# A decoder layer on one core: the mixer's steps in another order, weight splits and softmax scaling moved from GpSimd to VectorE, and one evacuation put behind the root

## The chip, the cores and the metric

The kernel runs on one NeuronCore of a Trainium2 chip. The metric is the device time of one execution in microseconds (us); the figure compared is the median of several runs. A profile of one execution shows when each instruction ran on TensorE (PE: matmuls; PEld: its weight loads), VectorE (DVE), ScalarE (ACT), GpSimd (POOL) and SyncE (SP, which issues the transfers).

## The reference

One layer on 256 tokens of width 1024, all in 32-bit floats:

```python
x = x + 0.5 * rmsnorm(swiglu(rmsnorm(x, g1), w_gate, w_up, w_down), post1)      # FFN 1, width 2816
h = rmsnorm(x, g2); q, k, v, p = split(h @ w_in)                                # 8 heads of 64, 512 pool channels
attn = softmax(q k^T / 8 - slope * (i - j), causal) v                           # 256 tokens are one block
pool = (mean of the last 2, 4, 8, 16 tokens - token) @ pool_w, * pool_scale     # 4 groups of 128 channels
x = x + rmsnorm([attn, pool] @ w_out, post2)
x = x + rmsnorm(cross_attention(rmsnorm(x, g3), rmsnorm(mem, g4)), post3)       # 4 heads of 256, 256 memory rows
x = x + 0.5 * rmsnorm(swiglu(rmsnorm(x, g5), ...), post4)                       # FFN 2
```

## The kernel before

All products with weights run as three matmuls of a rounded 32-bit kind: weights and activations are each split into a high part (rounded) and a low part (the rest), and high x high, high x low and low x high are added up in PSUM. The weights come as units of 8 tiles of 128x128, in the order in which they are used. `Weights._make` does a unit: ACT casts the raw unit to its high part (L79), and DVE or POOL subtracts it from the raw one (L80, the *split*, tiles `wlo<-wraw,whi`). In the FFNs every split is DVE's. Between them (mixer and cross-attention) every third unit, by `u % 3` (L76), goes to POOL, unless a written-out pace names the engine, as in the last seam. A unit is made four to five units ahead of its use.

PE's order is the order of the program. The other engines' order is found by a scheduler at build time, except in stretches between two `seam` marks, where it is the order of the code too. Each engine runs its instructions strictly in that order.

**The seams.** After each sub-layer's last product, the output's two halves of 512 columns lie in PSUM for each of two blocks of 128 tokens. `row_sums` (L312) squares each half on ACT (L322, with a sum) and multiplies it by a gain into `y` on DVE (L323). `row_root` (L328) takes the root on ACT (L330) and a reciprocal on DVE (L331). `row_add` (L338) adds y, scaled, to the residual `xt` on DVE (L339). PE transposes `xt` (L345), and ACT and DVE write the next input's high (L366, `x_hi`) and low halves (L370, `x_lo`). In the first two seams (into the mixer, into the cross-attention) PE has a pair of memory-key columns as filler between the transpositions; in the last one (into FFN 2) it has none, and the chain goes by small pieces (`ahead`, L413). Then a group of four column blocks starts (L230 low weights, L235 and L237 high weights with high and low input).

**The mixer** (from L867 on). A `pair` is two column blocks of `w_in` (L176 to L178) into the two halves of one PSUM bank (48 matmuls). After the query group, the order is: pool columns 15 and 14, the spread of the norm (L285, then `rBx`), pool columns 13 and 12, keys 4 and 5, keys 6 and 7. Then self-attention, between four blocks `vv` of the values' columns (L263 to L265): scores of two heads at a time (`self_scores`, L636, plain 32-bit float matmuls into two `small` PSUM buffers), their softmax (`self_softmax`: bias L643, maxima L645 and L646, L647, exponentials on ACT L648 and L649, and, put off to the next unit, reciprocal L652 and scaling L653 on DVE and L654 on POOL), the transposition of each head (`self_turn`, L660 to L662, copied by ACT, L663). `pool_windows` (L682) forms the trailing sums on POOL (L693 to L698), reading a DVE product (L686); `pool_out` multiplies by the pool weights (L703). The output projection `w_out` runs in eight steps (`row_step`, L297 to L299); `self_values` (L669, L671) of two heads stands behind each of the first four steps.

PSUM has eight banks: two `small`, six accumulators.

Of the kernel before, what the change touches and what calls it, by code (L numbers as in the profile page):

```python
# [15 lines left out]
P = 128  # L16
# [31 lines left out]
class Weights:  # L48
# [21 lines left out]
    def _make(self, u, engine=None):  # L70
        self._load(u)
        raw = self.raw[u]
        hi = self.pools["hi"].tile([P, UNIT * P], F32R, name="whi")
        lo = self.pools["lo"].tile([P, UNIT * P], F32R, name="wlo")
        if engine is None:
            ffn = self.tiles[u * UNIT][0].startswith("ffn")  # L76
            engine = "dve" if ffn or u % 3 else "pool"
        eng = self.nc.gpsimd if engine == "pool" else self.nc.vector
        self.nc.scalar.copy(hi, raw)  # L79
        eng.tensor_tensor(lo, raw, hi.bitcast(F32), op=ALU.subtract)  # L80
        self.split[u] = (hi, lo)
        self._load(u + 1)
        self._load(u + 2)
# [56 lines left out]
def build(nc, io, tiles_only=False):  # L140
# [170 lines left out]

    def row_sums(parts, ks, ws, t, factor):  # L312

        ys = st["ys"]
        s = tmp([P, 8], "fs")
        last = len(HALVES) - 1
        for i, d in enumerate(HALVES):
            for j, (k, w) in enumerate(zip(ks, ws)):
                row_product(parts(k), st["acc"], 0, False, j == len(ks) - 1, t, d, w)
            a = st["acc"][t][i]  # L320
            q = tmp([P, 512], "q")
            nc.scalar.activation(q, a, AF.Square, accum_out=s[:, i:i + 1])  # L322
            nc.vector.scalar_tensor_tensor(ys[:, t, d], a, factor, st["post"][:, d], op0=ALU.mult, op1=ALU.mult)  # L323
            if i == 0:
                nc.vector.tensor_scalar(s[:, 4:5], s[:, 0:1], 1.0 / D, EPS, op0=ALU.mult, op1=ALU.add)
        return s, last
# [33 lines left out]
    def row_end(parts, ks, weights, factor, nxt, pre, fillers):  # L360
# [12 lines left out]
        def products():  # L373
            st["w"].pace = [(LEAD, None)] * (LATE - 1) + [(LEAD - 1, None)]
            ws = [st["w"].get(UNIT) for _ in ks]
            st["w"].flush()
            st["ys"] = keep([P, 2, D], "y")
            r = row_root(row_sums(parts, ks, ws, 0, factor))
            st[nxt] = xsplit()
            st["xsum"] = tmp([P, 2, 2], "xsum")  # L380
            for d in HALVES:
                row_add(0, d, r)
            box["sums"] = row_sums(parts, ks, ws, 1, factor)
            x_turn(0, range(4), small)
            x_turn(0, range(4, 8), small)

        def middle():
# [6 lines left out]
            for c in range(ND):  # L394
                x_hi(0, c)
            for i in range(4):
                row_add(1, quarter(i), r)
# [15 lines left out]
        def ahead():  # L413
# [9 lines left out]
            x_lo(0, 1)  # L423
            x_lo(1, 1)

        def before(j):
# [202 lines left out]

    def self_scores(c):  # L630
        ps = [small("sc"), small("sc")]
        for lo, n, m in ((P, S, 0), (0, P, S)):
# [7 lines left out]
    def self_softmax(h, ps):  # L640
# [10 lines left out]
        def finish():  # L651
            nc.vector.reciprocal(m[:, 6:8], m[:, 4:6])  # L652
            nc.vector.tensor_scalar(s[:, :S], s[:, :S], m[:, 6:7], None, op0=ALU.mult)  # L653
            nc.gpsimd.tensor_tensor(s[:, S:], s[:, S:], m[:, 7:8].to_broadcast([P, P]), op=ALU.mult)  # L654
        defer(finish)
# [8 lines left out]

    def self_values(c):
        po, v = small("po"), st["v"]
        for h in (2 * c, 2 * c + 1):
# [14 lines left out]
    def pool_windows(g):  # L682
        W = S + PAD
        a = st["pin", g]
        aw = st["ps"][:, 4 + g, :S]
        nc.vector.tensor_tensor(a[:, PAD:], st["pps", g], st["rBx"], op=ALU.mult)  # L686
# [165 lines left out]
    def from_ffn1(parts, ks, weights):  # L852
        def to_mid():
# [14 lines left out]
    seam(False)  # L868
    pair("w_in", "xs_mix", [15 * P, 14 * P], lambda ps: (pool_in(3)(halves(ps)[0]), pool_in(2)(halves(ps)[1])),
         lambda: side(x_root))  # L870
    table(AF.Exp)
    side(x_spread)

    def q_out():
        pool_windows(3)
        pool_windows(2)
        for i, ps in enumerate(held["q"]):
            scaled_pair("qk", 2 * i, ps)

    def enter_mix():  # L880
# [3 lines left out]

    def pool_more(ps):
        for g in (1, 0):
            pool_in(g)(halves(ps)[1 - g])
            pool_windows(g)
    pair("w_in", "xs_mix", [13 * P, 12 * P], pool_more, lambda: side(q_out))
    for i in (4, 6):  # L890
        pair("w_in", "xs_mix", [i * P, (i + 1) * P], lambda ps, i=i: scaled_pair("qk", i, ps))
    side(self_scores, 0)
    fill(vv)
    side(self_scores, 1)
    fill(vv)
    side(self_turn, 0, accum)
    side(self_turn, 1, accum)
    fill(vv)
    side(self_scores, 2)
    fill(vv)  # L900
    side(self_scores, 3)
    side(self_turn, 2, accum)
    side(self_turn, 3, accum)
    side(pool_out, 3)
    k = K.pop(0)
    pr.add(*k[0])
    side(pool_out, 2)
    side(self_turn, 4)
    side(pool_out, 1)
    side(self_turn, 5)  # L910
    side(pool_out, 0)
# [9 lines left out]
    for j, k in enumerate(order[:ND - LATE]):  # L921
        pr.add(lambda k=k, j=j: row_step(st["xs_mixo"], k, j == 0), w_out(k))
        if j == 0:
            side(k_flush)
        if j < 4:
            side(self_values, j)
    seam(True)
# [167 lines left out]
```

## Time and profile before

| | us |
|---|---|
| median of 3 runs | 584.61 (583.85 to 585.74) |
| the profiled execution | 585.12 |
| its span, first to last instruction | 583.2 |
| PE busy | 569.8 (98%) |
| DVE busy | 397.3 (68%) |
| ACT busy | 341.4 (59%) |
| POOL busy | 68.8 (12%) |

PE's granted clock is full in all 40 slices of the span. The span and its 1.9 us surroundings make the execution's time. A busy share is a mean over all stages; what a wait of PE costs is read from PE's timeline at that place, where each row has start, duration, engine, line, tiles and, in brackets, the idle time of the engine ahead of it and what ended that.

### The profile page before, as it was taken

Reading aid. Unit: us, or ns where it says so; the run is one execution under the profiler, and the core shown is the slowest. Engines: PE = TensorE matmul, PEld = TensorE weight load, DVE = VectorE, ACT = ScalarE, POOL = GpSimd, SP = SyncE. Lnnn points to the kernel's source line nnn. Section 1 sums busy time; section 2 is a strip of 40 time slices with the busy share of each in tenths; the row PEclk is TensorE's granted clock in tenths of the full one; section 3 lists DMA queues with packets and bytes.
Section 4 is the critical chain, followed back from the end, with each engine's and each line's share of the span. In section 5 each row is a group of like instructions: output and inputs, shape, how many; then the busy total and the mean of one; then the engine's idle time right before and its main releaser. Section 6 shows DMA issues by size and latency. Waiting matters only on the chain.

```text
span 583.2 us, 8490 instructions
## 1 busy us (share of the span) xinstructions
PE 569.8 (98%) x3288; PEld 494.4 (85%) x3288; DVE 397.3 (68%) x634; ACT 341.4 (59%) x619; POOL 68.8 (12%) x63
## 2 busy tenths in 40 slices
PE   8999999999999999999999999999999999999995
PEld 7888888888888899778799988879888888888884
DVE  5499667777776857784377567367796766766654
ACT  6688665555555476476369457358674555555433
POOL 0000000000001126833214311101000000000001
PEclk9999999999999999999999999999999999999999
DMA  8986675556455346434336634426665555545402
GB/s 263 348 348 221 232 264 203 181 180 209 158 212 149 120 179 239 159 131 144 145 109 219 221 139 145 144 73 217 217 226 183 204 176 186 203 162 213 145 0 73
DMA packets 29833, 107.04 MB, mean 184 GB/s; under 512 B 2144, under 2 KB 3936, under 8 KB 29408
## 3 DMA queue, kind: packets, MB, share of 16 engines
q1 hardware_dynamic: 29360, 105.29, 51.7%
q10 hardware_dynamic: 432, 1.20, 0.6%
q8 instruction: 26, 0.43, 0.3%
q14 instruction: 15, 0.12, 0.1%
HBM read 105.44 MB, written 1.05 MB: 183 GB/s over the span
## 4 chain that ended last, share of the span: by engine, by line
PE 84%; ACT 4%; DMA 4%; DVE 3%; POOL 2%; issue 2%; SPq 0%; ACTq 0%; DVEq 0%; POOLq 0%
PE acc L550 13%; PE sm L550 12%; PE acc L297 10%; PE acc L298 10%; PE acc L299 10%; PE acc L549 6%; PE sm L549 6%; DMA wraw<-w 3%; ACT whi L79 2%; PE acc L176 2%; PE acc L178 2%; PE acc L177 2%; PE acc L263 1%; PE acc L265 1%; PE acc L264 1%
## 5 line engine op out<-in xcount | busy, mean ns | idle before, releaser
L80 DVE TENSOR_TENSOR wlo<-wraw,whi 128x1024 fp32r<-128x1024 f32 x164 | 204.9, 1253 | 82.6 <-ACT whi L79 82.2
L79 ACT CAST whi<-wraw 128x1024 fp32r<-128x1024 f32 x184 | 192.2, 1051 | 62.7 <-PE acc L299 36.9
L550 PE MATMUL acc<-xs,whi 128*128 128x512 f32 x320 | 114.6, 398 | 0.0
L550 PE MATMUL sm<-xs,whi 128*128 128x512 f32 x320 | 114.3, 397 | 0.0
L549 PE MATMUL acc<-xs,wlo 128*128 128x256 f32 x320 | 89.9, 281 | 0.4 <-DVE wlo L80 0.4
L549 PE MATMUL sm<-xs,wlo 128*128 128x256 f32 x320 | 90.0, 281 | 0.0
L80 POOL TENSOR_TENSOR wlo<-wraw,whi 128x1024 fp32r<-128x1024 f32 x20 | 48.7, 2435 | 313.9 <-ACT whi L79 300.0
L550 PEld LDWEIGHTS sm<-xs,whi 128*128 128x128 f32 x320 | 60.1, 188 | 14.8
L550 PEld LDWEIGHTS acc<-xs,whi 128*128 128x128 f32 x320 | 60.1, 188 | 14.3
L297 PE MATMUL acc<-whi,h 128*128 128x512 f32 x176 | 69.7, 396 | 0.0
L298 PE MATMUL acc<-wlo,h 128*128 128x512 f32 x176 | 69.5, 395 | 0.0
L299 PE MATMUL acc<-whi,h 128*128 128x512 f32 x176 | 69.3, 394 | 0.0
L549 PEld LDWEIGHTS acc<-xs,wlo 128*128 128x128 f32 x320 | 60.4, 189 | 2.1 <-DVE wlo L80 0.7
L549 PEld LDWEIGHTS sm<-xs,wlo 128*128 128x128 f32 x320 | 60.5, 189 | 0.0
L176 PE MATMUL acc<-xs,wlo 128*128 128x256 f32 x160 | 46.0, 288 | 0.0
L178 PE MATMUL acc<-xs,whi 128*128 128x256 f32 x160 | 45.3, 283 | 0.0
L177 PE MATMUL acc<-xs,whi 128*128 128x256 f32 x160 | 45.3, 283 | 0.0
L554 ACT COPY cmb<-sm 128x256 f32<-128x256 f32 x40 | 14.9, 371 | 48.8 <-PE sm L550 48.7
L554 ACT COPY cmb<-acc 128x256 f32<-128x256 f32 x40 | 14.9, 371 | 48.2 <-PE acc L550 47.9
L299 PEld LDWEIGHTS acc<-whi,h 128*128 128x128 f32 x176 | 33.0, 187 | 8.1
L298 PEld LDWEIGHTS acc<-wlo,h 128*128 128x128 f32 x176 | 33.0, 188 | 7.9
L297 PEld LDWEIGHTS acc<-whi,h 128*128 128x128 f32 x176 | 33.0, 188 | 6.6
(165 smaller groups left out, 935.4 us busy)
## 6 DMA issues: line engine op xcount, KB each, us to landing
wraw<-w SPq DMA_DIRECT2D x91, 1024.0 KB, 4.9
post<-post SPq DMA_DIRECT2D x4, 512.0 KB, 4.8
wraw<-w SPq DMA_DIRECT2D x7, 256.0 KB, 4.8
wraw<-w SPq DMA_DIRECT2D x2, 512.0 KB, 6.4
xt<-xt ACTq DMA_DIRECT2D x1, 1024.0 KB, 6.1
y<-memt SPq DMA_DIRECT2D x1, 1024.0 KB, 7.7
y<-mem SPq DMA_DIRECT2D x1, 1024.0 KB, 7.0
y<-x SPq DMA_DIRECT2D x7, 128.0 KB, 4.1
```

Source lines behind the costliest of these rows:

```text
L79: self.nc.scalar.copy(hi, raw)
L80: eng.tensor_tensor(lo, raw, hi.bitcast(F32), op=ALU.subtract)
L176: nc.tensor.matmul(o, lo, X[:, :S], start=first, stop=False, skip_group_check=True)
L177: nc.tensor.matmul(o, hi, X[:, :S], start=False, stop=False, skip_group_check=True)
L178: nc.tensor.matmul(o, hi, X[:, S:], start=False, stop=last, skip_group_check=True)
L263: nc.tensor.matmul(box[t], a, hi, start=k == 0, stop=False)
L297: nc.tensor.matmul(o, a, hi, start=first, stop=False, skip_group_check=True)
L298: nc.tensor.matmul(o, a, lo, start=False, stop=False, skip_group_check=True)
L299: nc.tensor.matmul(o, b, hi, start=False, stop=last, skip_group_check=True)
L549: nc.tensor.matmul(ps[:, S:], lo, x[:, :S], start=k == 0, stop=False, skip_group_check=True)
L550: nc.tensor.matmul(ps, hi, x, start=False, stop=k == ND - 1, skip_group_check=True)
L554: nc.scalar.copy(c, ps[:, S:])
```

## The change

Five parts:

1. Weight splits: the rule `u % 3` goes; without a named engine DVE does every split. The pace of the last seam still names POOL for one unit.
2. The scaling of the near half of a softmax (128x128) goes from POOL to DVE.
3. In the seams, for the second block of tokens, the evacuation of the second half into `y` is put off: behind the root and the first two row updates (seams with fillers), or behind the small pieces of `ahead` (last seam). The end of the kernel does not use it.
4. The mixer's order: keys first (4 and 5, then 6 and 7), scores of four heads in one visit, pool columns 15 and 14, the scores of the other four heads, pool columns 13 and 12, then the value blocks with the transpositions between them. All four groups of values stand in one visit behind the first step of `w_out`. The second two heads of each visit use accumulators instead of `small` buffers.
5. The pool's scaled copy gets two buffers of its own instead of a place in the softmax tile.

```diff
-        if engine is None:
-            ffn = self.tiles[u * UNIT][0].startswith("ffn")
-            engine = "dve" if ffn or u % 3 else "pool"
         eng = self.nc.gpsimd if engine == "pool" else self.nc.vector
...
-    def row_sums(parts, ks, ws, t, factor):
+    def row_sums(parts, ks, ws, t, factor, later=None):
...
-            nc.vector.scalar_tensor_tensor(ys[:, t, d], a, factor, st["post"][:, d], op0=ALU.mult, op1=ALU.mult)
+
+            def scaled(a=a, d=d):
+                nc.vector.scalar_tensor_tensor(ys[:, t, d], a, factor, st["post"][:, d], op0=ALU.mult, op1=ALU.mult)
+            if i == last and later is not None:
+                later.append(scaled)
+            else:
+                scaled()
...
-            for i in range(4):
+            for i in range(2):
+                row_add(1, quarter(i), r)
+            box["later"][0]()
+            for i in range(2, 4):
                 row_add(1, quarter(i), r)
...
-            nc.gpsimd.tensor_tensor(s[:, S:], s[:, S:], m[:, 7:8].to_broadcast([P, P]), op=ALU.mult)
+            nc.vector.tensor_scalar(s[:, S:], s[:, S:], m[:, 7:8], None, op0=ALU.mult)
...
-        aw = st["ps"][:, 4 + g, :S]
+        aw = st["self"].tile([P, S], F32, name="aw", bufs=2)
...
-    pair("w_in", "xs_mix", [15 * P, 14 * P], lambda ps: (pool_in(3)(halves(ps)[0]), pool_in(2)(halves(ps)[1])),
-         lambda: side(x_root))
+    pair("w_in", "xs_mix", [4 * P, 5 * P], lambda ps: held.update(k=ps), lambda: side(x_root))
...
+    side(q_out)
+    pair("w_in", "xs_mix", [6 * P, 7 * P], lambda ps: scaled_pair("qk", 6, ps))
+    side(self_scores, 0, small)
+    side(self_scores, 1, accum)
+    pool_pair(3)
+    side(self_scores, 2, small)
+    side(self_scores, 3, accum)
+    pool_pair(1)
     fill(vv)
     side(self_turn, 0, accum)
     side(self_turn, 1, accum)
     fill(vv)
-    side(self_scores, 2)
-    fill(vv)
-    side(self_scores, 3)
     side(self_turn, 2, accum)
     side(self_turn, 3, accum)
+    fill(vv)
     side(pool_out, 3)
+    side(pool_out, 2)
+    fill(vv)
+    side(self_turn, 4)
+    side(self_turn, 5)
...
         if j == 0:
             side(k_flush)
-        if j < 4:
-            side(self_values, j)
+            for c in range(4):
+                side(self_values, c, accum if c % 2 else small)
```

Three places show what that does to the engines' own order. The first is PE at the values: `po` and, in the changed kernel, `sm` and `acc` are the PSUM buffers of a group of two heads. Before, one group and then the next step of the projection:

```order
L299 MATMUL acc<-whi,xs 128x512
L669 MATMUL po<-ps,v 64x256
L671 MATMUL po<-ps,v 64x128
L669 MATMUL po<-ps,v 64x256
L671 MATMUL po<-ps,v 64x128
L297 MATMUL acc<-whi,xs 128x512
```

and of the change, two of the four groups that now follow each other:

```order
L678 MATMUL sm<-ps,v 64x256
L680 MATMUL sm<-ps,v 64x128
L678 MATMUL sm<-ps,v 64x256
L680 MATMUL sm<-ps,v 64x128
L678 MATMUL acc<-ps,v 64x256
L680 MATMUL acc<-ps,v 64x128
L678 MATMUL acc<-ps,v 64x256
L680 MATMUL acc<-ps,v 64x128
```

What moved: the other three groups came up to the first one, from behind the next three steps.

The second is DVE in the last seam, where `fs` is the root of the second block of tokens. Before:

```order
L323 SCALAR_TENSOR_TENSOR y<-acc,post 128x512
L331 RECIPROCAL fs<-fs 128x1
L339 SCALAR_TENSOR_TENSOR xt<-y,fs,xt 128x128 x2
L370 SCALAR_TENSOR_TENSOR xs<-sm,gain,xs 128x128
L339 SCALAR_TENSOR_TENSOR xt<-y,fs,xt 128x256
```

and of the change:

```order
L335 RECIPROCAL fs<-fs 128x1
L343 SCALAR_TENSOR_TENSOR xt<-y,fs,xt 128x128 x2
L374 SCALAR_TENSOR_TENSOR xs<-sm,gain,xs 128x128
L343 SCALAR_TENSOR_TENSOR xt<-y,fs,xt 128x256
L374 SCALAR_TENSOR_TENSOR xs<-acc,gain,xs 128x128
L374 SCALAR_TENSOR_TENSOR xs<-sm,gain,xs 128x128
L374 SCALAR_TENSOR_TENSOR xs<-acc,gain,xs 128x128
L323 SCALAR_TENSOR_TENSOR y<-acc,post 128x512
```

What moved: the evacuation `y` of the second half went from ahead of the reciprocal to behind the first low halves.

The third is DVE in the mixer, at the evacuation of the pool columns (`pin`, one group each; in the changed kernel `pin_2580` and `pin_2592` are those of columns 13 and 12). Before, the first two stand right behind the norm's spread, ahead of the queries' scaling:

```order
L80 TENSOR_TENSOR wlo<-wraw,whi 128x1024 x2
L686 TENSOR_TENSOR pin_2254<-acc,rBx 128x256
L686 TENSOR_TENSOR pin_2256<-acc,rBx 128x256
L801 TENSOR_TENSOR qk<-acc,rBx 128x512 x2
L80 TENSOR_TENSOR wlo<-wraw,whi 128x1024
L686 TENSOR_TENSOR pin_2354<-acc,rBx 128x256
```

and of the change, the last two, among the scalings of the last heads:

```order
L77 TENSOR_TENSOR wlo<-wraw,whi 128x1024
L661 RECIPROCAL mx<-mx 128x2 x2
L695 TENSOR_TENSOR pin_2580<-acc,rBx 128x256
L662 TENSOR_SCALAR ps<-ps,mx 128x256
L663 TENSOR_SCALAR ps<-ps,mx 128x128
L662 TENSOR_SCALAR ps<-ps,mx 128x256
L663 TENSOR_SCALAR ps<-ps,mx 128x128
L695 TENSOR_TENSOR pin_2592<-acc,rBx 128x256
```

What moved: the pool's evacuations now stand behind the softmax of the heads whose scores were formed ahead of them.

## Rows read from the trace of the kernel before

**Rows 1.** The page's costliest groups: name, tiles, count | busy us, mean ns | idle

```profile
L80 DVE TENSOR_TENSOR wlo<-wraw,whi 128x1024 fp32r<-128x1024 f32 x164 | 204.9, 1253 | 82.6 <-ACT whi L79 82.2
L79 ACT CAST whi<-wraw 128x1024 fp32r<-128x1024 f32 x184 | 192.2, 1051 | 62.7 <-PE acc L299 36.9
```

**Rows 2.** Timeline of PE in the mixer: start us, duration us, instruction, [idle before]

```profile
221.43 0.37 PE L176 MATMUL acc<-xs,wlo 128*128 128x256 f32 x1
...
238.88 0.92 PE L636 MATMUL sc<-qk 64*128 64x256 f32 x8
...
246.18 0.39 PE L265 MATMUL acc<-whi,xs 128*128 128x512 f32 x1
247.83 0.33 PE L660 MATMUL acc<-const,ps 128*128 128x128 f32 x1 [1.26 <-POOL ps L654]
...
255.40 0.39 PE L265 MATMUL acc<-whi,xs 128*128 128x512 f32 x1
256.52 1.38 PE L636 MATMUL sc<-qk 64*128 64x256 f32 x8 [0.74 <-DVE ps L643]
```

**Rows 3.** Timeline of PE at the first visit for the values

```profile
269.62 0.39 PE L298 MATMUL acc<-wlo,xs 128*128 128x512 f32 x1
269.85 0.39 PE L299 MATMUL acc<-whi,xs 128*128 128x512 f32 x1
270.16 0.66 PE L669 MATMUL po<-ps,v 128*64 128x256 f32 x4
...
270.97 0.50 PE L297 MATMUL acc<-whi,xs 128*128 128x512 f32 x1
271.31 0.40 PE L298 MATMUL acc<-wlo,xs 128*128 128x512 f32 x1
```

**Rows 4.** Timeline of PE at the three seams

```profile
204.29 0.39 PE L237 MATMUL acc<-xs,whi 128*128 128x256 f32 x1 [0.87 <-DVE xs L370]
...
301.50 0.34 PE L237 MATMUL acc<-xs,whi 128*128 128x256 f32 x1
...
388.82 0.56 PE L345 MATMUL acc<-const,xt 128*128 128x128 f32 x2 [1.18 <-DVE xt L339]
```

**Rows 5.** Timeline of DVE at the three seams

```profile
200.35 2.59 DVE L80 TENSOR_TENSOR wlo<-wraw,whi 128x1024 fp32r<-128x1024 f32 x1 [0.77 <-ACT whi L79]
...
297.75 2.35 DVE L80 TENSOR_TENSOR wlo<-wraw,whi 128x1024 fp32r<-128x1024 f32 x2
...
301.06 0.34 DVE L370 SCALAR_TENSOR_TENSOR xs<-acc,gain,xs 128x128 fp32r<-128x128 f32 x1
...
387.53 0.69 DVE L323 SCALAR_TENSOR_TENSOR y<-acc,post 128x512 f32<-128x512 f32 x1 [1.21 <-ACT q L322]
388.14 0.15 DVE L331 RECIPROCAL fs<-fs 128x1 f32<-128x1 f32 x1
388.32 0.61 DVE L339 SCALAR_TENSOR_TENSOR xt<-y,fs,xt 128x128 f32<-128x128 f32 x2
```

**Rows 6.** Timeline of POOL: two weight splits and a window step

```profile
199.45 2.41 POOL L80 TENSOR_TENSOR wlo<-wraw,whi 128x1024 fp32r<-128x1024 f32 x1 [14.22 <-ACT whi L79]
...
226.63 0.64 POOL L695 TENSOR_TENSOR win<-win 128x270 f32<-128x270 f32 x1
...
243.24 2.40 POOL L80 TENSOR_TENSOR wlo<-wraw,whi 128x1024 fp32r<-128x1024 f32 x1
```

**Rows 7.** Timeline of ACT at the last seam

```profile
387.53 0.29 ACT L330 ACTIVATE fs<-fs 128x1 f32<-128x1 f32 x1
```

**Rows 8.** Timeline of DVE in the softmax

```profile
243.40 2.26 DVE L647 TENSOR_SCALAR mx<-mx 128x2 f32<-128x2 f32 x1
...
255.92 1.01 DVE L643 SCALAR_TENSOR_TENSOR ps<-sc,const 128x384 f32<-128x384 f32 x2
...
258.15 0.55 DVE L643 SCALAR_TENSOR_TENSOR ps<-sc,const 128x384 f32<-128x384 f32 x1
...
259.45 0.34 DVE L653 TENSOR_SCALAR ps<-ps,mx 128x256 f32<-128x256 f32 x1
```

More of the change, by code (lines that the diff above doesn't have):

```diff
@@ L382, in products @@
                 row_add(0, d, r)
-            box["sums"] = row_sums(parts, ks, ws, 1, factor)
+            box["later"] = []
+            box["sums"] = row_sums(parts, ks, ws, 1, factor, box["later"])
             x_turn(0, range(4), small)
@@ L424, in ahead @@
             x_lo(1, 1)
+            box["later"][0]()
         def before(j):
@@ L626, in last_rows, with self_scores @@
         pr.add(run, weights)
-    def self_scores(c):
-        ps = [small("sc"), small("sc")]
+    def self_scores(c, alloc):
+        ps = [alloc(), alloc()]
         for lo, n, m in ((P, S, 0), (0, P, S)):
@@ L663, in self_turn, with self_values @@
         nc.scalar.copy(s, pt[:, :3 * P])
-    def self_values(c):
-        po, v = small("po"), st["v"]
+    def self_values(c, alloc):
+        po, v = alloc(), st["v"]
         for h in (2 * c, 2 * c + 1):
@@ L874, in q_out @@
     def q_out():
-        pool_windows(3)
-        pool_windows(2)
         for i, ps in enumerate(held["q"]):
             scaled_pair("qk", 2 * i, ps)
+        scaled_pair("qk", 4, held["k"])
     def enter_mix():
@@ L883, in build, with pool_pair, done @@
     side(enter_mix)
[L885 to L892, printed above, removed]
-    fill(vv)
-    side(self_scores, 1)
+    def pool_pair(g):
+        def done(ps):
+            for i in (g, g - 1):
+                pool_in(i)(halves(ps)[g - i])
+                pool_windows(i)
+        pair("w_in", "xs_mix", [(12 + g) * P, (11 + g) * P], done)
+    side(q_out)
[6 more added lines that the diff above has]
+    pool_pair(1)
     fill(vv)
@@ L898, in build @@
     fill(vv)
-    side(self_scores, 2)
-    fill(vv)
-    side(self_scores, 3)
     side(self_turn, 2, accum)
     side(self_turn, 3, accum)
+    fill(vv)
     side(pool_out, 3)
+    side(pool_out, 2)
+    fill(vv)
+    side(self_turn, 4)
+    side(self_turn, 5)
     k = K.pop(0)
     pr.add(*k[0])
-    side(pool_out, 2)
-    side(self_turn, 4)
     side(pool_out, 1)
-    side(self_turn, 5)
     side(pool_out, 0)
```

## The prediction
> **What bounds the kernel now.** I read the page first: TensorE (PE) is busy in every slice and its granted clock is full, so the time is PE's own work plus the few places where PE waits. I then listed PE's waits by length and opened the timeline of PE around each, and of the engine that ended it. The costliest groups give two prices used throughout: a weight unit costs ScalarE (ACT) 1.05 us for the cast and VectorE (DVE) 1.25 us for the split [rows 1].
>
> The mixer holds the two longest waits that this change can touch [rows 2]. The first transposition of a head begins at 247.83, 1.65 us after the last matmul ahead of it (246.18); its wait ended on GpSimd's (POOL's) scaling of that head. The last score visit begins at 256.52, 1.12 us after 255.40; it waited for a PSUM buffer that DVE had not yet read. Between 32-bit float matmuls and the rounded ones there is also a price for each crossing [rows 3]: matmuls of 512 columns follow each other at 0.23 us, but the values begin 0.31 us after the last one (269.85 to 270.16), and the one that comes after them takes 0.34 (270.97 to 271.31). A visit thus costs at least 0.08 + 0.11 = 0.19 us beside its own work. Then the seams [rows 4]: PE waits 0.87 us for DVE at 204.29, nearly nothing at 301.50, and 1.18 at 388.82.
>
> **Mix seam, at 200.** Before the first product that needs the low half, DVE works through four low halves, the splits, four more low halves and one more. Here one of two splits is POOL's, and DVE's own took 2.59 us instead of 1.25, ending 1.08 us after POOL's (199.45 + 2.41 = 201.86) [rows 5, 6]. In the next seam both splits are DVE's: from 297.75 to the end of the low half at 301.40, 3.65 us [rows 5]. The change makes the first seam like the second. DVE was free at 200.35 - 0.77 = 199.58; the deferred half of y (below) makes that 199.93, plus 3.65 is 203.58. PE follows such a low half by 0.05 to 0.1 (301.40 to 301.50), so it starts at about 203.63 instead of 204.29. Gain 0.66; bounds 0.3 and the wait itself, 0.87.
>
> **Half of y behind the root.** Before, DVE starts y (387.53), and the reciprocal stands behind it at 388.14, though ACT's root was done at 387.53 + 0.29 = 387.82 [rows 5, 7]. With y moved, the reciprocal can start at about 387.86, 0.28 us earlier, and in the last seam the first row update (388.32) and PE's 388.82 come 0.28 earlier; y then fits into DVE's idle time before the next high halves. In the two seams with fillers the same move costs: DVE now stands idle for the root (0.29 + 0.04) while y, 0.61 us, stays in front of the low halves. The end of the chain is about 0.33 later. In the mix seam this is counted above; in the next one PE's 301.50 followed 301.40 at once, so it is lost: +0.30 there (bounds 0 and 0.35). The other move of that seam, a third split on DVE before the first y, finds DVE idle.
>
> **Mixer order and POOL.** Scaling on DVE stands right behind the reciprocal. In the new order a head's transposition comes a whole pool pair and more after its softmax: three pairs take 238.88 - 221.43 = 17.45 us, so a pair is 5.8 [rows 2]. The POOL queue, with 2.4 us splits in front of the scaling, is gone: the 1.65 us go back to 0.31, -1.34. The scores use four buffers at a visit (two small, two accumulators), and the second visit is a pair later: 1.12 to 0.31, -0.81. Visits: eleven before (four scores, one merged with transpositions; three more with transpositions; four values), nine now. Two fewer at 0.19 is -0.38, at most twice that with the slower first and last matmul of a visit; I take -0.4.
>
> **Load of DVE.** Nineteen splits (one stays with POOL by a written-out order in the last seam) and eight scalings come to DVE, 19 x 1.25 = 24 us over some 210 us. Part of that is given back. At 243.40 DVE took 2.26 us for a 128x2 multiplication, ending with POOL's split (243.24 + 2.40), where two score rows of 384 columns took 1.01 together [rows 6, 8]. In the cross-attention DVE's cost is hidden: PE has no wait there, and a unit is made four to five ahead of its use, some 11 to 13 us.
>
> The Trainium skill, page "SBUF — State Buffer", section "Who interferes with whom", states that a DVE instruction of two SBUF inputs, or of a 2-port mode such as tensor_scalar, and a GpSimd one exclude each other, "the loser fully blocks". This trace agrees, with 2.26 us for the small multiplication and 2.59 for the split. By that rule the gain from POOL's splits stands, but the pooling windows stay on POOL and now run during the softmax and its new scaling on DVE; that is the second rival.
>
> **Sum.** -0.66 - 0.28 + 0.30 - 1.34 - 0.81 - 0.40 = -3.19. The profiled execution took 585.12 us (span 583.2 and 1.9 around it): 581.93. It lay 0.51 above the median of 584.61, so 581.4 us.
>
> **Rivals.** *A new wait in the transpositions.* The fourth head's transposition needs the accumulator of the second pool pair, which DVE frees only with its last evacuation of it, behind eight softmaxes. PE's way from the first score to there: 2 x (1.8 + 5.8) for scores and pairs, two value blocks of 12 x 0.23 + 0.2, a transposition visit and a half (about 1.5): 22.7 us. DVE's way: a cast and a split stand in front, 2.3; then per four heads two blocks of 2.23 (255.92 to 258.15), four scalings of some 0.6 (0.34 for the wide one) [rows 8], a split and two evacuations of 0.35: 2 x 9.0 = 18. Slack 2.4 us. Some 13 DVE instructions in that stretch exclude POOL's window steps of 0.64 us [rows 6]; half a step each is 4 us if POOL never rests, 2 if it rests half the time. So the wait lies between 0 and 1.6; with 1.2 the time is 582.6. For it: the order; against: the share of POOL's rest.
>
> *DVE becomes the bound of the mixer, slower.* The same place: if DVE stands for POOL's windows nearly in full (14 wide steps of 0.64 and small ones, some 10 us) instead of interleaving, it comes 10 us late, less 2.4 of slack: +7.6, or 589. It decides from a lateness of 2.4 + 3.2 + 1.75 = 7.3 us on. For it speaks that DVE took 2.26 us for a 128x2; against, that this was one long POOL instruction, while window steps are short and let DVE in between.
>
> *The waits only move.* The 2.15 us of the two mixer waits reappear at another buffer or transposition, since the same softmax must be done by the same DVE. Then only seams and visits are left, -1.04: 583.6. Against it: the new order puts some 15 us between a score and its use, the old one had 5 to 9.
>
> **How the numbers follow.** Forecast 581.4: 0.62; new wait 582.6: 0.18; only moved 583.6: 0.13; DVE bound 589: 0.07. About 0.3%, 1.75 us, can be told from no change, so faster means below 582.86. The forecast's own bounds (mix seam 0.3 to 0.87, lost seam 0 to 0.35, visits 0.2 to 0.8) give 580.5 to 582.0, and the runs scatter by about 0.9 either way: 579.9 to 582.8 for it alone. Adding the third case, 579.9 to 583.7. Faster: 0.60 + 0.12 + 0.03 = 0.75; same 0.17; slower 0.08.
>
> **What would show it.** Right: no PE wait over 0.3 us between the end of the query group and the last seam; PE's 0.87 in the mix seam down to about 0.2; a new one of 0.3 in the next seam; 1.18 in the last one down to 0.9; no DVE multiplication of 128x2 above 1 us. Wrong: a PE wait at the transpositions that ends on DVE's pool evacuation (first rival), PE waiting for weight splits or scores with DVE without idle time (second), or PE waits of 2 us in the mixer that end on other buffers (third). The visits are wrong if the sum of PE's time from the first score to the end of the values, waits taken off, does not fall by 0.2 us or more.

## The result and the profile after

The changed kernel took 579.51 us (median of 4 runs, 578.48 to 579.67) beside 585.11 for the kernel before (583.85 to 585.74): ratio 0.9901 [0.9886, 0.9916], faster by 5.6 us. The forecast was 581.4, a gain of 3.2 us, with a range of 579.9 to 583.7: the direction was right, the gain is some 1.75 times the forecast one, and the time lies 0.4 us below the range. The profiled execution took 579.55 us, span 577.6.

First the waits of PE over the whole span: line, what it waited for, us in total, times, longest.

```profile
PE warm L476 <- DVE cmb L473: 1.2, 1, 1.2
PE acc L232 <- ACT whi L108: 1.0, 1, 1.0
PE acc L349 <- DVE xt L343: 0.9, 1, 0.9
PE acc L558 <- DVE wlo L77: 0.7, 1, 0.7
PE acc L234 <- DVE xs L374: 0.5, 2, 0.3
PE acc L227 <- ACT xs L370: 0.2, 1, 0.2
```

Neither of the two mixer waits is left: no line is a transposition (L669 now) or a score (L645). The first two and the fourth line lie at the start and in the first FFN; the third and the last are the last seam; the fifth is one wait of 0.25 us in each of the other two seams. PE's timeline in the mixer shows the same (start us, duration us; it answers to [rows 2]).

```profile
234.01 0.28 PE L175 MATMUL acc<-xs,whi 128*128 128x256 f32 x1
234.22 0.92 PE L645 MATMUL sm<-qk 64*128 64x256 f32 x8
234.97 0.82 PE L645 MATMUL acc<-qk 64*128 64x256 f32 x8
...
244.09 0.39 PE L262 MATMUL acc<-whi,xs 128*128 128x512 f32 x1
244.32 0.27 PE L669 MATMUL acc<-const,ps 128*128 128x128 f32 x1
...
247.50 0.39 PE L262 MATMUL acc<-whi,xs 128*128 128x512 f32 x1
247.73 0.27 PE L669 MATMUL acc<-const,ps 128*128 128x128 f32 x1
```

A transposition starts 0.23 us after the matmul ahead of it, the spacing of two matmuls of 512 columns; before it was 1.65. The second score visit, now behind matmuls of 256 columns, starts 0.21 us after the last of them; the late one before started 1.12 us after its own.

The one visit for all values (answers to [rows 3]):

```profile
265.23 0.39 PE L296 MATMUL acc<-whi,xs 128*128 128x512 f32 x1
265.55 0.66 PE L678 MATMUL sm<-ps,v 128*64 128x256 f32 x4
...
268.35 0.50 PE L294 MATMUL acc<-whi,xs 128*128 128x512 f32 x1
268.69 0.40 PE L295 MATMUL acc<-wlo,xs 128*128 128x512 f32 x1
```

The same gap of 0.32 ahead and the same 0.34 after the first matmul behind it, but once instead of four times.

The seams, PE (answers to [rows 4]):

```profile
203.18 0.28 PE L232 MATMUL acc<-xs,whi 128*128 128x256 f32 x1
203.71 0.39 PE L234 MATMUL acc<-xs,whi 128*128 128x256 f32 x1 [0.25 <-DVE xs L374]
...
295.54 0.28 PE L232 MATMUL acc<-xs,whi 128*128 128x256 f32 x1
296.07 0.39 PE L234 MATMUL acc<-xs,whi 128*128 128x256 f32 x1 [0.25 <-DVE xs L374]
...
383.15 0.56 PE L349 MATMUL acc<-const,xt 128*128 128x128 f32 x2 [0.91 <-DVE xt L343]
```

The wait of 0.87 is down to 0.25, the next seam has a new one of 0.25, and the last one went from 1.18 to 0.91. The brackets are a little smaller than the loss: from 295.54 to 296.07 are 0.53 us where such matmuls follow each other at 0.12, so the new wait costs 0.41.

DVE at the places of [rows 5, 8]:

```profile
200.00 2.36 DVE L77 TENSOR_TENSOR wlo<-wraw,whi 128x1024 fp32r<-128x1024 f32 x2
...
240.27 0.44 DVE L656 TENSOR_SCALAR mx<-mx 128x2 f32<-128x2 f32 x1
...
243.57 0.77 DVE L663 TENSOR_SCALAR ps<-ps,mx 128x128 f32<-128x128 f32 x1
...
247.51 0.41 DVE L695 TENSOR_TENSOR pin<-acc,rBx 128x256 f32<-128x256 f32 x1
247.84 7.29 DVE L77 TENSOR_TENSOR wlo<-wraw,whi 128x1024 fp32r<-128x1024 f32 x5
...
382.45 0.16 DVE L335 RECIPROCAL fs<-fs 128x1 f32<-128x1 f32 x1 [1.54 <-ACT fs L334]
...
384.67 0.68 DVE L323 SCALAR_TENSOR_TENSOR y<-acc,post 128x512 f32<-128x512 f32 x1
```

Both splits of the mix seam now run together at 1.18 us each. The multiplication of 128x2, which took 2.26, takes 0.44 at most; a scaling (L663) up to 0.77. In the last seam DVE waits for the root and y comes behind the small pieces.

And POOL, which still does the pooling windows:

```profile
243.39 0.86 POOL L707 TENSOR_TENSOR pin<-win,aw 128x256 f32<-128x256 f32 x1
...
247.88 1.77 POOL L707 TENSOR_TENSOR pin<-win,aw 128x256 f32<-128x256 f32 x1
249.61 1.59 POOL L704 TENSOR_TENSOR win<-pin 128x256 f32<-128x256 f32 x1
```

Beside the run of splits that DVE begins at 247.84, window steps stretch to 1.6 to 1.8 us, and the five splits take 1.46 each instead of 1.2. So the two still hold each other up. It costs nothing: PE waits for neither.

**Where the time went.** I cut PE's timeline at the first matmul of each sub-layer's first group. The stretch from the mixer's query group to the cross-attention's one (the *mixer stretch*) fell from 98.24 to 92.36 us; the one from there to FFN 2 rose from 88.76 to 88.93; the rest behind it, to PE's last matmul, takes 186.91 in both. The stretch ahead of the mixer took 194.59 and 194.73. The sum, -5.57, is all but 0.1 us of the difference of the spans (583.2 and 577.6). Within the mixer stretch, by kind of work (times from one PE start to the next):

| us | before | after | splits alone (below) |
|---|---|---|---|
| query group, high halves (mix seam) | 8.81 | 8.19 | 7.73 |
| value columns | 13.95 | 11.40 | 11.72 |
| scores | 3.87 | 3.02 | 3.41 |
| transpositions of the heads | 3.07 | 2.29 | 2.51 |
| values | 3.23 | 2.80 | 3.23 |
| output projection | 22.94 | 22.14 | 22.94 |
| pairs of columns | 35.23 | 35.40 | 35.24 |
| all (with the small rest) | 98.24 | 92.36 | 93.91 |

### The profile page after: what moved, and what is told of

It is laid out like the page before. It is cut to its first block, busy times and chain, and to the rows that moved or that the text cites. A ratio compares the mean times of both kernels' runs of the same rounds, so it can differ in the third digit from the quotient of the medians.

```text
span 577.6 us, 8466 instructions
## 1 busy us (share of the span) xinstructions
PE 566.6 (98%) x3288; PEld 494.8 (86%) x3288; DVE 406.4 (70%) x661; ACT 342.0 (59%) x619; POOL 20.0 (3%) x36
## 3 DMA queue, kind: packets, MB, share of 16 engines
HBM read 105.44 MB, written 1.05 MB: 184 GB/s over the span
## 4 chain that ended last, share of the span: by engine, by line
PE 91%; DVE 3%; DMA 3%; ACT 1%; issue 1%; SPq 1%; DVEq 0%; ACTq 0%
PE acc L559 13%; PE sm L559 13%; PE acc L294 10%; PE acc L295 10%; PE acc L296 10%; PE acc L558 6%; PE sm L558 6%; DMA wraw<-w 3%; PE acc L173 3%; PE acc L174 3%; PE acc L175 3%; PE acc L234 2%; PE acc L232 2%; PE acc L260 2%; PE acc L262 2%; PE acc L261 2%
## 5 line engine op out<-in xcount | busy, mean ns | idle before, releaser
L77 DVE TENSOR_TENSOR wlo<-wraw,whi 128x1024 fp32r<-128x1024 f32 x183 | 223.9, 1231 | 84.2 <-ACT whi L76 83.8
L175 PE MATMUL acc<-xs,whi 128*128 128x256 f32 x160 | 45.2, 283 | 0.0
L174 PE MATMUL acc<-xs,whi 128*128 128x256 f32 x160 | 45.2, 283 | 0.0
L232 PE MATMUL acc<-xs,whi 128*128 128x256 f32 x128 | 33.6, 292 | 1.0 <-ACT whi L108 1.0
```

The lines of the kernel that those rows point to most:

```text
L174: nc.tensor.matmul(o, hi, X[:, :S], start=False, stop=False, skip_group_check=True)
L175: nc.tensor.matmul(o, hi, X[:, S:], start=False, stop=last, skip_group_check=True)
L232: nc.tensor.matmul(o[i], hi, st[X][:, k, :S], start=first and i % 2 == 0, stop=False, skip_group_check=True)
```

## The experiments

Stretches are compared rather than whole times where one run stands for a kernel. The stretch ahead of the mixer has the same work in all these kernels but ranges from 194.2 to 198.6 us, while the mixer stretch of the changed kernel came out at 92.36 and 92.35 in two profiles.

**The values step by step** (changed kernel, values back to four visits)

```diff
-        if j == 0:
-            for c in range(4):
-                side(self_values, c, accum if c % 2 else small)
+        if j < 4:
+            side(self_values, j, small)
```

> The changed kernel, but the four groups of values stand behind the first four steps of the output projection again, one each, all in small buffers. Measure: the stretch from PE's first matmul of the query group to its first one of the cross-attention's query group (98.24 us before the change, 92.36 after). Theory: a visit of matmuls with 64 rows of 32-bit floats costs 0.41 us beside its own work, so three more visits give 92.36 + 1.23 = 93.6. Rival, the prediction's price of 0.19: 92.9.

Mixer stretch 93.57, +1.21 for three more visits: 0.40 each, as the theory had it. PE's timeline at the second of the four visits:

```profile
273.15 0.39 PE L296 MATMUL acc<-whi,xs 128*128 128x512 f32 x1
273.47 0.66 PE L678 MATMUL sm<-ps,v 128*64 128x256 f32 x4
```

It waits for nothing, and pays the gap of 0.32 anew, as each of the four does. Its one time, 584.91 us, is no verdict on the values: PE waited 2.4 and 2.1 us for weights in the first FFN, where the changed kernel waited 0.7 and 1.0.

**The scores apart** (changed kernel; the second scores of each visit between the halves of the pool pair)

```diff
...
-    side(self_scores, 1, accum)
-    pool_pair(3)
+    pool_pair(3, lambda: side(self_scores, 1, accum))
...
-    side(self_scores, 3, accum)
-    pool_pair(1)
+    pool_pair(1, lambda: side(self_scores, 3, accum))
```

> The changed kernel, but the scores are formed in four visits of two heads again: the second and the fourth stand between the halves of the two pool pairs. Theory (0.41 us a visit): 92.36 + 0.82 = 93.2 for the same stretch, and no wait of PE in the mixer, as DVE is not late. Rival (0.19): 92.7. Second rival: the later scores push the softmax of the second heads behind the pool's evacuation, and PE waits at the transpositions: over 94.

Mixer stretch 93.10, +0.74 for two visits, 0.37 each; one run, 580.03 us. No wait of PE came into the mixer. The theory holds; 92.7 and a wait at the transpositions do not.

**The engines alone** (kernel before, splits and scaling on DVE, old order, y as before)

```diff
-        if engine is None:
-            ffn = self.tiles[u * UNIT][0].startswith("ffn")
-            engine = "dve" if ffn or u % 3 else "pool"
...
-            nc.gpsimd.tensor_tensor(s[:, S:], s[:, S:], m[:, 7:8].to_broadcast([P, P]), op=ALU.mult)
+            nc.vector.tensor_scalar(s[:, S:], s[:, S:], m[:, 7:8], None, op0=ALU.mult)
```

> The kernel before, with its order, but all weight splits (save the one that the last seam names) and the softmax scaling on DVE. Theory: POOL's long splits made all of the mixer's waits, in front of the scaling in POOL's queue and by holding DVE up, so 3.16 us of waits go and the mix seam gains 0.99 (no deferred y here): the stretch of 98.24 becomes 94.1, the time 581.0. Rival: the old order itself leaves DVE too little time between scores and transposition, half of the waits stay: 95.7, 582.5.

580.87 us (580.49 to 581.56), ratio 0.9922 [0.9905, 0.994]; mixer stretch 94.24, close to the theory's 94.1 and far from the rival's 95.7.

**The order alone** (changed kernel with the splits' rule and the scaling back on POOL, and y in its old place)

```diff
+        if engine is None:
+            ffn = self.tiles[u * UNIT][0].startswith("ffn")
+            engine = "dve" if ffn or u % 3 else "pool"
...
-            box["sums"] = row_sums(parts, ks, ws, 1, factor, box["later"])
+            box["sums"] = row_sums(parts, ks, ws, 1, factor)
...
-            nc.vector.tensor_scalar(s[:, S:], s[:, S:], m[:, 7:8], None, op0=ALU.mult)
+            nc.gpsimd.tensor_tensor(s[:, S:], s[:, S:], m[:, 7:8].to_broadcast([P, P]), op=ALU.mult)
```

> The new order of the mixer alone: every third weight split and the softmax scaling stay on POOL, and y is not put off. Theory: distance between scores and transpositions hides POOL too, so the 3.16 us of waits go, and five fewer 64-row visits less three more of transpositions give 1.75: the stretch is 98.24 - 3.16 - 1.75 = 93.3, the time 580.2. Rival: POOL's queue (splits, windows and scaling in one line) comes late for the transpositions, and PE waits 1 to 3 us there: 94.3 to 96.3.

581.19 us (579.77 to 582.58), ratio 0.9925 [0.9896, 0.9954]; mixer stretch 92.97, with no wait in it but the 0.9 us of the mix seam: 0.3 better than the theory, and the rival's waits did not come. Engines alone gave -4.00 and order alone -5.27; both together give -6.35 with y in its old place there (91.89, the next run; -5.88 with the late y). The two overlap: each clears the mixer's two long waits by itself. The order alone keeps part 5 of the change too; no run has that part by itself.

**y late in the last seam only** (changed kernel; the two seams with fillers as before)

```diff
-            box["sums"] = row_sums(parts, ks, ws, 1, factor, box["later"])
+            box["sums"] = row_sums(parts, ks, ws, 1, factor, None if fillers else box["later"])
...
-            for i in range(2):
-                row_add(1, quarter(i), r)
-            box["later"][0]()
-            for i in range(2, 4):
+            for i in range(4):
                 row_add(1, quarter(i), r)
```

> The changed kernel, but the second half of y is put off only in the last seam; in the two seams with fillers it stands ahead of the root as before. Theory: there the deferral only made DVE idle for the root (0.29 + 0.04 us) and so delayed the low halves: from the mixer's query group to the cross-attention's 92.36 - 0.33 = 92.0 us, from there to the FFN's group 88.93 - 0.42 = 88.5, the whole some 0.8 us faster than the changed kernel. Rival: the deferral is neutral or a gain there too: 92.4 or more and 88.9.

578.87 us (577.78 to 579.99), ratio 0.9885 [0.9862, 0.9907]; mixer stretch 91.89, the next one 88.50, both as expected. The deferral therefore costs 0.47 us in the mix seam and 0.43 in the next one, and only the last seam gains by it (88.76 - 88.50 = 0.26).

**A transposition apart** (a control on the changed kernel: the fourth head's transposition one value block later, in front of a pool product)

```diff
-    side(self_turn, 3, accum)
     fill(vv)
+    side(self_turn, 3, accum)
     side(pool_out, 3)
...
```

> The changed kernel, but the fourth head's transposition stands one value block later than the third's, together with the pool products: the transpositions and pool products have the same number of visits, the last head only changes its visit. Control: theory and rival both expect 92.36 + 0.0 to 0.1 for the stretch; a change over 0.3 would mean that a transposition in a visit of pool products costs a crossing of its own.

Mixer stretch 92.32 beside 92.36; one run, 580.08 us. The time does not hang on where this transposition stands.

**Fewer visits still** (on top of *y late in the last seam only*: transpositions four to a visit, the values right behind the last ones)

```diff
+    fill(vv)
     side(self_turn, 0, accum)
     side(self_turn, 1, accum)
+    side(self_turn, 2)
+    side(self_turn, 3)
     fill(vv)
-    side(self_turn, 2, accum)
-    side(self_turn, 3, accum)
     fill(vv)
     side(pool_out, 3)
     side(pool_out, 2)
-    fill(vv)
     side(self_turn, 4)
     side(self_turn, 5)
...
+    pr.add(*k[1])
+    table(AF.Sqrt)
     side(pool_out, 1)
     side(pool_out, 0)
-    pr.add(*k[1])
-    table(AF.Sqrt)
     side(self_turn, 6)
     side(self_turn, 7)
+    for c in range(4):
+        side(self_values, c, small if c > 1 else accum)
...
-            for c in range(4):
-                side(self_values, c, accum if c % 2 else small)
```

> The kernel of e5 with fewer visits: four transpositions together behind the second value block, the first pool products with heads 4 and 5, the second ones with heads 6 and 7 and, right behind them, all values ahead of the projection's first step. Four visits fewer, three of them of transpositions or pool products. Theory: those cost 0.2 us, the one of values 0.3 to 0.4, and no wait comes in: 92.0 - 1.0 = 91.0 for the stretch, the time some 1.8 us under the changed kernel. Rival: with the transpositions bunched, the copies on ACT come late and PE waits 0.5 us or more at the second bunch or at the values: 91.5 or above.

578.16 us (577.41 to 580.85), ratio 0.9882 [0.9859, 0.9905]; mixer stretch 91.76. The expectation failed: four visits fewer gained 0.13 us, not 0.9. No new wait ate it. By kind, the projections and columns fell by 0.8 us, and the pool products (+0.37) and transpositions (+0.26) rose. These are times to the next start, and most of that only moved: four pool matmuls with a transposition behind them take 0.86 us (253.05 to 253.91), with columns behind them 0.67 and another 0.19 at the first of the columns. And the values start 0.20 us after a transposition, where the next one would follow at 0.11: they pay their 0.09 there as behind the projection (0.32 for 0.23). So merging transpositions and pool products saves next to nothing, and a values visit merged with them keeps its gap; what saved here is scores beside scores and values beside values.

**The changed kernel again** (no edit), on the same chip as *fewer visits still* and *y late in the last seam only*

> The changed kernel once more, beside e5 and e7 on one chip. Both theories: the stretch 92.36, the next one 88.93, and a ratio to the kernel before near 0.99; e5 and e7 are measured against it.

580.11 us (579.18 to 581.55), ratio 0.9908 [0.9887, 0.9929], mixer stretch 92.35. On this chip the two versions with y late in the last seam only lie 1.2 us (578.87) and 2.0 us (578.16) lower, and so beat both kernels; from each other they can't be told apart. In the profiles 0.9 and 1.05 us of that lie in the mixer stretch and the next one; the rest lies ahead of them, where two profiles of the changed kernel differ as much (194.73 and 195.85).

**The splits alone** (kernel before, only the rule removed)

```diff
-        if engine is None:
-            ffn = self.tiles[u * UNIT][0].startswith("ffn")
-            engine = "dve" if ffn or u % 3 else "pool"
```

> The kernel before with one edit: all weight splits (save the last seam's named one) on DVE, the softmax scaling still on POOL. Of the 4.0 us that both moves gave on the old order (98.24 to 94.24 in the stretch), the mix seam holds 1.1 and the mixer's waits 2.9. Theory: POOL's long splits did nearly all of it, by queueing ahead of the scaling and by holding DVE's small multiplication up: 94.2 to 94.6. Rival: the scaling on POOL is itself the late part: 95.5 or above.

Mixer stretch 93.91 (one run, 581.44 us), 0.3 us better than the theory's range and 1.6 below its rival: this part by itself clears every wait of the mixer, and with it the mix seam's. PE's timeline at the places of [rows 2]:

```profile
245.52 0.39 PE L262 MATMUL acc<-whi,xs 128*128 128x512 f32 x1
245.75 0.27 PE L657 MATMUL acc<-const,ps 128*128 128x128 f32 x1
...
248.94 0.39 PE L262 MATMUL acc<-whi,xs 128*128 128x512 f32 x1
249.26 0.92 PE L633 MATMUL sc<-qk 64*128 64x256 f32 x8
```

POOL's scaling, on which the old wait ended, was still there. What held it up in the kernel before was not POOL's queue. DVE and POOL in that kernel:

```profile
247.13 0.16 DVE L652 RECIPROCAL mx<-mx 128x2 f32<-128x2 f32 x1
...
247.37 0.40 POOL L654 TENSOR_TENSOR ps<-ps,mx 128x128 f32<-128x128 f32 x1 [1.74 <-DVE mx L652]
```

POOL's split had ended at 243.24 + 2.40 = 245.64 [rows 6], and POOL stood idle for 1.74 us until DVE's reciprocal; it did so, for shorter or longer, ahead of all eight scalings. The reciprocal was late because DVE's multiplication took 2.26 us beside POOL's split [rows 8]. Here it is:

```profile
242.74 0.15 DVE L644 TENSOR_SCALAR mx<-mx 128x2 f32<-128x2 f32 x1
```

From DVE's read of the scores to the reciprocal are 5.51 us in the kernel before (241.62 to 247.13) and 3.44 here (240.96 to 244.40). The difference of 2.07 matches what the multiplication lost, 2.11. So this wait came by way of DVE. At the scores' wait another multiplication had taken 1.87 us beside a POOL split (249.29); the steps from there to the late read at 255.92 were not taken apart, but without the splits that wait is gone too. The theory's other cause, splits queueing ahead of the scaling, is not in the trace.

**The scaling alone** (kernel before, only the scaling's line changed)

```diff
-            nc.gpsimd.tensor_tensor(s[:, S:], s[:, S:], m[:, 7:8].to_broadcast([P, P]), op=ALU.mult)
+            nc.vector.tensor_scalar(s[:, S:], s[:, S:], m[:, 7:8], None, op0=ALU.mult)
```

> The kernel before with the other edit: the softmax scaling on DVE, every third split still on POOL. Theory: DVE is still held up by POOL's splits (2.26 and 1.87 us for a 128x2 multiplication), so the mix seam keeps its wait and most of the mixer's waits stay: 97 to 98. Rival (the POOL queue alone made the waits): 95.3, as then 2.9 go and only the seam's 1.1 stays.

Mixer stretch 102.09 (one run, 590.15 us): *slower* than before by 3.85 us. Neither theory nor rival had that. DVE, and then POOL, in that kernel:

```profile
244.70 2.27 DVE L647 TENSOR_SCALAR mx<-mx 128x2 f32<-128x2 f32 x1
...
249.20 0.28 DVE L654 TENSOR_SCALAR ps<-ps,mx 128x128 f32<-128x128 f32 x1
...
250.05 2.36 DVE L654 TENSOR_SCALAR ps<-ps,mx 128x128 f32<-128x128 f32 x1
```

```profile
244.55 2.40 POOL L80 TENSOR_TENSOR wlo<-wraw,whi 128x1024 fp32r<-128x1024 f32 x1
249.94 2.38 POOL L80 TENSOR_TENSOR wlo<-wraw,whi 128x1024 fp32r<-128x1024 f32 x1 [3.00 <-ACT whi L79]
```

The same scaling takes 0.28 us alone and 2.36 when a POOL split has begun 0.11 us ahead of it; it ends 0.09 us after the split. PE waits for a scaling twice:

```profile
249.54 0.33 PE L660 MATMUL acc<-const,ps 128*128 128x128 f32 x1 [1.66 <-DVE ps L654]
...
252.47 0.47 PE L660 MATMUL acc<-const,ps 128*128 128x128 f32 x1 [2.38 <-DVE ps L654]
```

The first is the old wait, 0.4 us longer: the multiplication loses 2.1 us beside a split as before, and the scaling of 0.28, now DVE's, starts 0.79 us after its reciprocal (248.41) with a read of scores and the wide scaling in between, where POOL began it after 0.24. The second is the scaling of 2.36.

And there is a second bill. By stretch (start:end, length, PE busy and instructions, granted clock, DMA share, GB/s):

```profile
248.00:250.00 2.00, 0.46 (x3) 1.00 0.69 276
250.00:252.00 2.00, 0.08 (x1) 0.81 0.62 252
252.00:254.00 2.00, 1.53 (x5) 0.50 0.36 31
...
256.00:258.00 2.00, 2.00 (x6) 0.50 0.28 115
258.00:260.00 2.00, 2.00 (x14) 0.98 0.00 0
```

After 4 us with only 0.54 us of work, PE came back at a granted clock of 0.50 (1.2 instead of 2.4 GHz) and kept it to about 258: the block of twelve matmuls behind the waits took 5.26 us where it took 2.94 before. So 2.3 us of the loss are the clock and not the wait itself.

**A pool product apart** (changed kernel; the last pool product one step of `w_out` later, away from the other)

```diff
         side(pool_out, 1)
-        side(pool_out, 0)
...
+        if j == 1:
+            side(pool_out, 0)
```

> The changed kernel with one more visit of another kind: the last pool product (plain 32-bit floats too, but 128 rows in and out) stands alone behind the projection's second step. Theory A, the crossing costs because the matmuls are plain 32-bit floats: 92.36 + 0.35 to 0.4 = 92.7. Theory B, it is the 64-row shape of scores and values that costs: 92.36 + 0.1 or less.

Mixer stretch 92.35 (one run, 579.29 us), the same as with both in one visit. The theory that every crossing between plain 32-bit matmuls and rounded ones costs 0.35 us or more falls. PE there:

```profile
270.21 0.40 PE L296 MATMUL acc<-whi,xs 128*128 128x512 f32 x1
270.44 0.59 PE L712 MATMUL acc<-pin,poolw 128*128 128x256 f32 x2
270.68 0.58 PE L294 MATMUL acc<-whi,xs 128*128 128x512 f32 x1
271.10 0.40 PE L295 MATMUL acc<-wlo,xs 128*128 128x512 f32 x1
```

The pool product starts 0.23 us after the matmul ahead of it, without a gap; values and scores start 0.32 and 0.21 us after matmuls that usually follow each other at 0.23 and 0.12. Two pool matmuls cost 0.43 either way: 0.24 at their place and 0.19 at the next matmul. That scores and values have operands of 64 rows or columns would fit; what in their shape costs the time is open.

**The scaling back on POOL** (changed kernel, that line the other way)

```diff
-            nc.vector.tensor_scalar(s[:, S:], s[:, S:], m[:, 7:8], None, op0=ALU.mult)
+            nc.gpsimd.tensor_tensor(s[:, S:], s[:, S:], m[:, 7:8].to_broadcast([P, P]), op=ALU.mult)
```

> The changed kernel with the softmax scaling back on GpSimd; the weight splits stay on DVE and the new order stays. Stretch from the mixer's query group to the cross-attention's one, 92.36 us with scaling on DVE. Theory (the scaling has a whole pool pair of slack in the new order, and without the splits GpSimd's queue holds only window steps of up to 1.8 us): no PE wait at a transposition, stretch 92.3 to 92.5 us, so this part of the change is worth nothing here. Rival (the scaling now queues behind GpSimd's window steps, and part 2 of the change was needed): a PE wait at a transposition that ends on the GpSimd line of the scaling, stretch 92.8 us or more.

Mixer stretch 92.34 (one run, 580.41 us), no wait in it. POOL in the middle of its window steps:

```profile
246.89 3.49 POOL L663 TENSOR_TENSOR ps<-ps,mx 128x128 f32<-128x128 f32 x4
```

These four scalings, of the last four heads, take 0.87 us each, and their heads are transposed from 254.79 on in the changed kernel. In the new order PE's time does not hang on the scaling's engine; in the old one the move to DVE costs. DVE gains by the scaling on POOL: its last evacuation of the pool columns (L695, 247.00 + 0.41) ends 1.23 us ahead of PE's fourth head (248.64); in the changed kernel the same distance is 0.14.

## Why the prediction was off

The signs that the prediction named for waits and seams all came (no wait in the mixer, 0.25 and 0.25 in the first two seams, 0.91 in the last one, no multiplication of 128x2 above 0.45 us). They told where the gain would come from and not how large it is. Each term of the sum, with what the runs gave:

| term | forecast | measured | from |
|---|---|---|---|
| mix seam, y late included | -0.66 | -0.62 | before, after |
| next seam, y late | +0.30 | +0.43 | after, y in the last seam only |
| last seam, y early behind the root | -0.28 | -0.26 | before, y in the last seam only |
| waits of the mixer | -2.15 | -3.25 | before, splits alone |
| visits | -0.40 | -2.02 | splits alone, y in the last seam only |
| sum | -3.19 | -5.72 | the profiles: -5.71 in the two stretches |

**The step that failed is the one on visits**: "eleven before (...), nine now. Two fewer at 0.19 is -0.38". It counted all visits alike. Scores fell from four visits to two and values from four to one, five fewer; the added visits were transpositions and pool products. The first kind costs 0.37 to 0.40 us each (measured by putting two and three of them back), the second hardly anything (the pool product apart, and the bunching that gained 0.13). 3 x 0.40 and 2 x 0.37 are 1.95 of the 2.02. What makes the price of scores and values is open. The price was also half of what it is: the step took the gap ahead of the values and the one slow matmul behind them from [rows 3], 0.19, and left out the visit's own start (four values visits take 3.23, the merged one 2.80: 0.14 for each that goes) and the later matmuls of the block behind, slower together by the remaining 0.07.

**The waits were undersized** by 1.1 us. The two terms, 1.34 and 0.81, were the first wait of a visit, and they were right: the two blocks of value columns ahead of them took 4.30 and 3.77 against 2.94, 2.19 together. But the second head of the same transposition visit and the second score of the same score visit waited too, inside it: the transpositions took 1.13 us instead of 0.57, and the scores that began at 256.52 took 1.31 instead of 0.85. That is the other 1.0. [Rows 2] held the second of these (1.38 beside 0.92); the first is this row of the kernel before, 0.38 us after the matmul ahead of it (248.23), where 0.11 is usual:

```profile
248.61 0.33 PE L660 MATMUL acc<-const,ps 128*128 128x128 f32 x1
```

**What made the waits** was named wrong, and that the first ones came out in size is luck. The term of 1.34 rests on "The POOL queue, with 2.4 us splits in front of the scaling, is gone". There was no such queue: POOL was idle ahead of the scaling, and DVE was late, held up by POOL's split (splits alone). The prediction had that row, 2.26 us for a small multiplication, but used it for the load of DVE and for a rival, not for the wait. Taking the splits off POOL would end a queue as well as a hold-up, and so the size came out. The other term, 0.81, was put down to four buffers and a later visit; the splits alone clear that wait with two buffers and in its old place. The slack of the new order clears both waits too, without the engines (order alone). The scaling, which the prediction counted as part of the cure, does nothing for PE in the new order; in the old one it costs 3.85 us by itself and still 0.33 with the splits on DVE (94.24 against 93.91), where the second head of a transposition visit starts 0.39 us after the matmul ahead of it instead of 0.11.

**The seams** came out within 0.13 us. Late y is a loss of 0.9 us in the two seams with fillers together; the prediction saw the sign in the second seam and hid the first in the sum of the mix seam, where without it the gain is 1.08.

**The rivals.** The new wait at the fourth head's transposition did not come, but barely: DVE's last evacuation of the pool pair ended at 247.51 + 0.41 = 247.92, and PE's fourth head starts at 248.06 (three matmuls behind 247.73 at 0.11). Of the reckoned slack of 2.4 us 0.14 was left. (The terms as written add up to 22.6 us for PE's way and 8.8 for four heads on DVE, a slack of 2.7.) With the scaling on POOL 1.23 is left, so some 1.1 went to the scalings on DVE; how the rest divides between the exclusion and the reckoning, no run separates. DVE as the bound did not come: beside short window steps no softmax instruction lost more than 0.5 us (L663, 0.77 instead of 0.28). That the waits only move is refuted by the list of waits. As to the range: its lowest bound, 580.5, less the scatter of 0.9 is 579.6 and not 579.9; the measured 579.51 lies below either.

## What to carry over

Read a wait's cost as the time of the whole visit against an undisturbed one; the first instruction's idle time leaves out the waits inside. Count the places where work alternates by kind of work, and price each kind from a place where it stands alone. Two edits that clear the same wait don't add up, so try them apart: here one rule removed in the old order gives three quarters of the gain (4.33 of 5.71 us), and another part alone is a loss that the rest covers. And look at what the engine that a wait ends on was itself waiting for: here POOL was named, and DVE was late.

## What the runs showed of the chip

- An instruction of 128x128 on DVE that takes 0.28 us took 2.36 beside a POOL one of 2.38; beside window steps of up to 0.9 us a scaling lost at most 0.5. In these rows the loss goes with the length of the one instruction on the other engine.
- TensorE's granted clock fell to 0.50 (1.2 GHz) by the end of two waits of 1.66 and 2.38 us close together, and stayed there for some 5.5 us in which PE was busy again; around the wait of 1.26 us in the kernel before it stayed at 1.00 (246 to 250).
- In the first FFN, whose code is nearly the same in all kernels, PE's wait for a low half of weights was 0.4 us in the profile of the kernel before, 0.7 in that of the changed one and 2.5 in that of its repetition: the whole time of a single run can't show an effect of 2 us.
